# Hybrid mLSTM and S5 decoder layer: the input products of an S5 unit issued ahead of the output products of the unit before it, and the mLSTM inputs taken through DRAM

## The chip, the cores and the metric

One core of one Trainium2 chip runs the whole layer in one launch. The metric is the device time of that launch in microseconds (us). Engines are named as the profile names them: PE (TensorE, matrix products), PEld (its weight loads), DVE (VectorE), ACT (ScalarE), POOL (GpSimd), SP (SyncE, which issues the DMAs).

## The reference

A layer of a decoder with 1024 features works on 1024 prompt positions and on 32 sample positions (8 rows of 4). Cut to what the change touches, it computes:

```
a = rmsnorm(h)
x_m, z_m, o_m, i, f, x_s, z_s = split(a @ w_in)     # 512 columns each; i and f have 4
x_conv = silu(causal_conv(x_m, width 4))
q, k from x_conv; v from x_m                        # 4 heads of 128, one matrix each
hA = mlstm_chunkwise(q, k, v, i, log_sigmoid(f))    # running maximum m, matrix memory C
hA = layernorm(hA * sigmoid(o_m)); hA = (hA + skip * x_conv) * silu(z_m)
yB = Re(C . scan(lam, B . x_s)) + D * x_s           # 32 groups of 16 channels, 64 complex states
yB = gelu(yB); yB = yB * sigmoid(yB @ w_glu + b) * silu(z_s)
h  = h + concat(hA, yB) @ w_out
h  = h + sigmoid(h @ w_ple_gate) * rmsnorm(p @ w_ple)
y  = rmsnorm(h)
```

It also returns the last states of the mLSTM, of the convolution and of the S5 scan.

## The kernel before

Features stand on the partitions and positions on the free axis: 1024 + 32 = 1056 columns, cut into chunks of 256, 384 and 416. A large product is made of three f32r matmuls for each block of 128 rows (`mm3`), the weight being split into a rounded part `hi` (cast on ACT, L115) and the rest `lo` = raw - hi (L116, on the engine that `lo_engine` names). So a tile of 128 output features costs 8 x 3 matmuls for each of three chunks, 72 in all. Such tiles are called after their piece of the input projection: `ps_o`, `ps_zm`, `ps_xm`, `ps_zs`, `ps_xs`.

The program has these stages: loading and normalising the input, the `xs` tiles, the S5 stage, the transition to the mLSTM (convolution, value products), the four heads of the mLSTM, the GLU, the output projection and the gate with the final norm.

**The S5 stage** (L916 to L950). The order of PE is written by hand there (`tc.manual_schedule`); everywhere else, and on all other engines, a scheduler sets it. Eight units of four channel groups each run one after the other. `s5_in(u)` builds a table `wt` on DVE and transposes it to `WV`. `s5_out(u)` builds `cs`, multiplies it (`kp`), writes the result to DRAM (`dK`) and reads it back as the Toeplitz tile `tz`. `s5_rot(u)` makes the rotations `rtr`, `rti` on DVE. `s5_run(u)` makes the input products `vr`, `vi` (16 matmuls of 144 columns, L616), rotates and scans them on DVE (`w`, `zr`, `zi`, `v`, `xs_`), makes the output products `py` (L654 and L655) from `tz` and `xs_`, and then the GELU (`sq`, `y`) and eight DMA writes to `d_y`. Between these pieces PE takes matmuls from a filler, a generator of tiles (`o_rest`, then `zm` 0 to 3, then `xm` 0 and 1), by a count of columns: `FILL_A` after the input products, `FILL_B` after the output products, `FILL_C` at the unit's end.

In the first four units a generator for the mLSTM's gates takes a step each: `tpr` on PE, sums and running maxima on DVE, `ends` to DRAM and back as `er`, a scan `mc`, `mc` to DRAM and back as `mp`, then `M`, `nM` and `nML` on DVE, `wl` on ACT, and the transposes `tpk` and `tps` on PE. These stand at the end of unit 3 in PE's order.

**The transition and the heads.** `mtile_xm(h)` brings `xm` of head h: for h = 0 and 1 it is read back from `d_xm`, where the filler wrote it, for h = 2 and 3 it is computed on the spot. Then come the convolution (`xc`, ACT L1059 and DVE L1061), the value products `vps`, and `mlstm(h)`, which begins with `qps` (L1099) and, on POOL, with a mask added to `nmb` (L1095). `glu_w` splits the GLU's weights (`hi_g` on ACT, `lo_g` on POOL, L966). `mlstm(h)` runs over two halves, each with one `qps`, so that the fifth `qps` begins head 2. The four `zs` tiles are held back by `tc.issue_after` until the last matmul of `xm` 3; they run among the heads 1 to 3.

Of the kernel before, what the change touches and what calls it, by code (L numbers as in the profile page):

```python
# [21 lines left out]
GC = 0.044715  # L22
NEG = -1.0e30
CH = ((0, 256), (256, 384), (640, 416))
FILL_A, FILL_B, FILL_C = 16500, 3600, 4400
LOC = tuple((c, 128 * (i - b)) for i, (c, b) in enumerate(((0, 0),) * 2 + ((1, 2),) * 3 + ((2, 5),) * 4))


# [1 line left out]
def tile_hymba(ctx: ExitStack, tc: tile.TileContext, d: dict, o: list):  # L30
# [535 lines left out]
    def s5_out(u):  # L566
        gs = slice(4 * u, 4 * u + 4)
        cs = s5.tile([128, 4, 9, 16], F32, tag="cs", name="cs", bufs=2)
        table(cs, Cs, Cj, 9, gs)
        yield  # L570

        kp = pt([128, 128], "kp")
        for i in range(4):
            g = 4 * u + i
            T.matmul(kp[32 * i:32 * i + 32, :], Bs[:, g:g + 2, :].rearrange("p q c -> p (q c)"),
                     cs[:, i, 0:8, :].rearrange("p t c -> p (t c)"), start=True, stop=True)
        ks = s5.tile([128, 128], F32, tag="ks", name="ks", bufs=1)
        A.copy(ks, kp)
        V.scalar_tensor_tensor(ks[:, 0:16], dsel, Dt[:, u:u + 1], ks[:, 0:16], op0=MUL, op1=ADD)
        dma(dK[u, :, :, 128:256].rearrange("r i x -> i r x"), ks)  # L580

        tz = pxm.tile([128, 4, 128], F32, tag="xm", name="tz", bufs=2)
        k0 = dK[u, 0:1, 0:1, 16:17]
        dma(tz, bass.AP(tensor=k0.tensor, offset=k0.offset, ap=[[16, 8], [256, 64], [1, 128]]))
        yield cs, tz
# [16 lines left out]
            V.tensor_tensor(dst, dst, u3, op=op)  # L602
        return rtr, rti

    def s5_run(u, WV, cs, tz, rtr, rti):
        q0 = 2 * u
        gb = 4 * (u % 2)
        us = s5.tile([128, 4, 144], F32, tag="us", name="us", bufs=2)
        dma(us, d_us[u // 2].rearrange("s c g n -> (s c) g n")[:, gb:gb + 4])
        y2 = s5.tile([128, 4, 128], F32, tag="y2", name="y2", bufs=1)  # L610
        vr, vi = pv([128, 2, 144], "vr"), pv([128, 2, 144], "vi")
        for x, v_ in enumerate((vr, vi)):
            for q in range(2):
# [236 lines left out]


    xsm = mlc.tile([128, 4, 8, 7], F32, name="xsm")
    d_xm = dram.tile([2, 128, 1024], F32, name="d_xm")

    def xm_g(h):
        hi, lo = wtile(wcols(128 * h, 128), 8, 128, f"xm{h}")
# [10 lines left out]

    def filler():
        yield from o_rest()
        for h in range(4):  # L870
            yield from z_tile_g(512 + 128 * h, h, f"zm{h}", s5)
        for h in range(2):
            yield from xm_g(h)

    fill = filler()

# [39 lines left out]
    with tc.manual_schedule(engines={mybir.EngineType.PE}):  # L916
        gate = gates_g()
        ins = [s5_in(u) for u in range(8)]
        outs = [s5_out(u) for u in range(8)]

        prod(ins[0])
        WV = prod(ins[0])
        prod(outs[0])
        nxt = prod(outs[0])
        with tc.high_priority():
            rot = s5_rot(0)
        prod(outs[1])
        for u in range(8):
            run = s5_run(u, WV, *nxt, *rot)
            prod(run)  # L930
            if u < 7:
                nxt = prod(outs[u + 1])
                prod(ins[u + 1])
            take(FILL_A)
            prod(run)
            take(FILL_B)
            if u < 7:
                WV = prod(ins[u + 1])
                with tc.high_priority():
                    rot = s5_rot(u + 1)  # L940
            prod(run)
            if u < 6:
                prod(outs[u + 2])
            take(FILL_C)
            if u < 4:
                next(gate)
        end = s5_final()
        for n in (5000, 3000, 3000, 1 << 30):
            prod(end)
            take(n)  # L950
    lo_engine[0] = G
# [7 lines left out]
    def glu_w():  # L959
        for k in range(0, 4, 2):  # L960
# [2 lines left out]
            hi = pgw.tile([128, 2, 512], F32R, name=f"hi_g{k}")  # L963
            lo = pgw.tile([128, 2, 512], F32R, name=f"lo_g{k}")
            A.copy(hi, raw)
            G.tensor_tensor(lo, raw, hi.bitcast(F32), op=SUB)  # L966
            wg.extend((hi[:, i, :], lo[:, i, :]) for i in range(2))

    mX = {}
# [68 lines left out]
    def mtile_xm(h):  # L1038
        xm = pxm.tile([128, 1027], F32, tag="xm", name="xm", bufs=2)
        V.memset(xm[:, 0:3], 0.0)  # L1040
        if h < 2:
            dma(xm[:, 3:], d_xm[h])
        else:
            hi, lo = wtile(wcols(128 * h, 128), 8, 128, f"xm{h}")

        def evac(c, t0, n, ps):
            n8 = min(n, 1024 - t0)
            A.copy(xm[:, 3 + t0:3 + t0 + n8], ps[:, :n8])
            if c == 2:
                A.copy(xsm[:, h, :, 3:7], ps[:, 384:416].rearrange("p (b t) -> p b t", t=4))  # L1050

        V.tensor_copy(xsm[:, h, :, 0:3], scT[:, h, :].rearrange("p (b j) -> p b j", j=3))
        if h > 1:
            mtile(hi, lo, evac, "xm")
        V.tensor_copy(pcn[:, h, 0:24].rearrange("p (b j) -> p b j", j=3), xsm[:, h, :, 4:7])
        V.tensor_copy(pcn[:, h, 24:27], xm[:, 1024:1027])

# [295 lines left out]
    glu_w()  # L1353
    mlstm(0, *xmc[0])
    mlstm_first(1)
    xmc[2] = mtile_xm(2)
    sample_head(2)
    xmc[3] = mtile_xm(3)
    xm_end = last_mm[0]
    with tc.high_priority():  # L1360
        sample_head(3)
    mlstm(2, *xmc[2])
    mlstm(3, *xmc[3])
    sample_end()
# [239 lines left out]
```

## Time and profile before

| what | us |
|---|---|
| median of three runs | 690.73 (690.07 to 693.43) |
| the profiled execution | 690.1 |
| its span | 688.4 |
| PE busy | 619.6 (90% of the span) |
| DVE busy | 449.6 (65%) |
| ACT busy | 266.7 (39%) |
| POOL busy | 167.5 (24%) |

The span runs from the first to the last instruction that the profile shows; 1.7 us of the execution's own time lie around it. The busy shares are averages over stages that differ: the S5 stage runs from about 103 to 252 us, the transition to 273, the heads and the GLU to 455, the output projection and the gate to the end.

### The profile page before, as it was taken

The page shows a single profiled execution, that of the slowest core. Times are in us where ns is not written, and L with a number is a line of the kernel's source. Part 1 is how long each engine was busy: PE and PEld are TensorE (multiplying, and loading weights), DVE is VectorE, ACT ScalarE, POOL GpSimd, SP SyncE. Part 2 cuts the span into 40 slices and gives each one's busy share as a digit, 9 for nine tenths or more (in the row PEclk, how much of TensorE's full clock was granted, in tenths as well). Part 3 has the DMA queues.
Part 4 walks back from the last instruction along what each step waited for, and adds up shares of the span by engine and source line. Part 5 has one row for each costly group of instructions (what it writes and reads, how often), then busy time and mean ns, then how long its engine had stood idle before and what let it go on. Part 6 is the DMA issues. An engine that isn't in the chain of part 4 may idle for free.

```text
span 688.4 us, 11569 instructions
## 1 busy us (share of the span) xinstructions
PE 619.6 (90%) x4068; PEld 544.8 (79%) x4068; DVE 449.6 (65%) x1289; ACT 266.7 (39%) x655; POOL 167.5 (24%) x173
## 2 busy tenths in 40 slices
PE   3999997987989963899899997799999999999995
PEld 2999997976988952789798896676888876788885
DVE  4878867897899648748766688945211334556344
ACT  5653732233433243434543245345111324353232
POOL 5820200000000005434443336573110214101000
PEclk9999998998999995899999999799999999999998
DMA  8812445344444528214545257467531246313121
GB/s 278 235 46 45 116 118 130 103 121 105 74 114 118 147 52 248 62 47 131 172 142 154 78 172 221 125 199 252 188 122 62 92 167 226 119 49 122 44 80 61
DMA packets 110831, 88.43 MB, mean 128 GB/s; under 512 B 33391, under 2 KB 93443, under 8 KB 110774
## 3 DMA queue, kind: packets, MB, share of 16 engines
q1 hardware_dynamic: 110774, 87.70, 43.1%
q8 instruction: 32, 0.52, 0.3%
q14 instruction: 25, 0.20, 0.1%
HBM read 61.14 MB, written 26.54 MB: 127 GB/s over the span
## 4 chain that ended last, share of the span: by engine, by line
PE 57%; DVE 17%; DMA 14%; ACT 4%; issue 4%; SPq 2%; POOL 1%; POOLq 0%; DVEq 0%; ACTq 0%
PE po L1425 4%; PE po L1424 4%; PE po L1532 4%; PE po L1423 4%; PE po L1533 4%; PE po L1534 4%; SPq L36 2%; DVE xc L1061 2%; PE ps_o L123 2%; DMA Wraw<-in_w_out 2%; PE ps_o L125 2%; PE ps_o L124 2%; PE ps_xm L123 2%; PE ps_xm L125 2%; PE ps_xm L124 2%
## 5 line engine op out<-in xcount | busy, mean ns | idle before, releaser
L1532 PE MATMUL po<-wgh,hTh 128*128 128x512 f32 (+1 forms) x136 | 52.3, 386 | 0.3 <-ACT g_t L1535 0.3
L1534 PE MATMUL po<-wgh,hTl 128*128 128x512 f32 (+1 forms) x136 | 51.1, 380 | 0.0
L1533 PE MATMUL po<-wgl,hTh 128*128 128x512 f32 (+1 forms) x136 | 51.1, 378 | 0.0
L1426 DVE TENSOR_TENSOR xt<-xt,po 128x512 f32<-128x512 f32 x16 | 11.0, 686 | 55.7 <-PE po L1425 52.2
L123 PE MATMUL ps_o<-hi_o,aTh 128*128 128x264 f32 (+2 forms) x136 | 41.7, 307 | 0.6 <-ACT aTh L178 0.6
L124 PE MATMUL ps_o<-lo_o,aTh 128*128 128x264 f32 (+2 forms) x136 | 40.4, 298 | 1.4 <-POOL lo_o L116 1.4
L125 PE MATMUL ps_o<-hi_o,aTl 128*128 128x264 f32 (+2 forms) x136 | 40.6, 298 | 0.2 <-DVE aTl L179 0.2
L123 PE MATMUL ps_xm<-aTh,hi_xm 128*128 128x256 f32 (+2 forms) x96 | 32.4, 337 | 1.4 <-ACT hi_xm L115 1.4
L1425 PE MATMUL po<-woh,mlo 128*128 128x512 f32 x80 | 32.8, 410 | 0.0
L123 PE MATMUL ps_zm<-aTh,hi_zm 128*128 128x256 f32 (+2 forms) x96 | 32.6, 340 | 0.0
L125 PE MATMUL ps_zs<-aTh,lo_zs 128*128 128x256 f32 (+2 forms) x96 | 32.3, 337 | 0.0
L124 PE MATMUL ps_zs<-aTl,hi_zs 128*128 128x256 f32 (+2 forms) x96 | 32.3, 336 | 0.0
L123 PE MATMUL ps_xs<-aTh,hi_xs 128*128 128x256 f32 (+2 forms) x96 | 31.4, 327 | 0.9 <-ACT xs L287 0.9
L1424 PE MATMUL po<-wol,mh 128*128 128x512 f32 x80 | 32.1, 402 | 0.0
L123 PE MATMUL ps_zs<-aTh,hi_zs 128*128 128x256 f32 (+2 forms) x96 | 32.0, 333 | 0.0
L124 PE MATMUL ps_xm<-aTl,hi_xm 128*128 128x256 f32 (+2 forms) x96 | 31.9, 333 | 0.0
L1423 PE MATMUL po<-woh,mh 128*128 128x512 f32 x80 | 31.7, 397 | 0.0
L125 PE MATMUL ps_xm<-aTh,lo_xm 128*128 128x256 f32 (+2 forms) x96 | 31.7, 332 | 0.0
L124 PE MATMUL ps_xs<-aTl,hi_xs 128*128 128x256 f32 (+2 forms) x96 | 31.4, 327 | 0.0
L124 PE MATMUL ps_zm<-aTl,hi_zm 128*128 128x256 f32 (+2 forms) x96 | 31.4, 327 | 0.0
L125 PE MATMUL ps_zm<-aTh,lo_zm 128*128 128x256 f32 (+2 forms) x96 | 31.3, 326 | 0.0
L125 PE MATMUL ps_xs<-aTh,lo_xs 128*128 128x256 f32 (+2 forms) x96 | 31.2, 325 | 0.0
(594 smaller groups left out, 1970.6 us busy)
## 6 DMA issues: line engine op xcount, KB each, us to landing
xt<-in_x_prompt SPq DMA_DIRECT2D x15, 512.0 KB
Wraw<-in_w_out SPq DMA_DIRECT2D x16, 256.0 KB
Wraw<-in_w_ple_gate SPq DMA_DIRECT2D x16, 256.0 KB
d_h<-xt SPq DMA_DIRECT2D x8, 512.0 KB
h_t<-d_h SPq DMA_DIRECT2D x8, 512.0 KB
out<-g_t SPq DMA_DIRECT2D x14, 256.0 KB
mt<-d_m SPq DMA_DIRECT2D x10, 256.0 KB
d_us<-xs SPq DMA_DIRECT2D x32, 72.0 KB
```

Source lines behind the costliest of these rows:

```text
L36: nc.sync.dma_start(out, in_)
L123: T.matmul(ps, wh, xh, start=first, stop=False)
L124: T.matmul(ps, wh, xl, start=False, stop=False)
L125: last_mm[0] = T.matmul(ps, wl, xh, start=False, stop=last).ins
L1061: V.scalar_tensor_tensor(xc, xm[:, j:j + 1024], cvw[:, 4 * j + h:4 * j + h + 1], xc, op0=MUL, op1=ADD)
L1423: T.matmul(ps, mh[:, k % 4, :], hi, start=k == 4, stop=False)
L1424: T.matmul(ps, mh[:, k % 4, :], lo, start=False, stop=False)
L1425: T.matmul(ps, mlo[:, k % 4, :], hi, start=False, stop=k == 3)
L1426: V.tensor_tensor(xt[:, cs], xt[:, cs], ps, op=ADD)
L1532: T.matmul(ps[:, :b - a], hTh[i][:, k, :], hi[:, ws], start=k == 4, stop=False)
L1533: T.matmul(ps[:, :b - a], hTh[i][:, k, :], lo[:, ws], start=False, stop=False)
L1534: T.matmul(ps[:, :b - a], hTl[i][:, k, :], hi[:, ws], start=False, stop=k == 3)
```

## The change

In the S5 stage the input products of unit u+1 are put into PE's order in the middle of unit u's filler, ahead of the output products of unit u; `kp` of unit u+1 stands with them. `s5_run` gets a yield after the input products for that, and a third `us` buffer. `tz` gets a buffer of its own instead of sharing that of `xm`. All four `xm` go through `d_xm`. The filler's order is `o_rest`, `xm` 0, `xm` 1, `zm` 0 to 3, `xm` 2; `xm` 3 is computed after `mlstm_first(1)`. The three column counts change. The `zs` tiles are no longer held back. `lo_engine` stays DVE after the S5 stage, and `lo_g` moves to DVE too, so that eight `lo` of 128x1024 (`xm` 2, `xm` 3, four `zs`, two `lo_g`) leave POOL for DVE.

```diff
-FILL_A, FILL_B, FILL_C = 16500, 3600, 4400
+FILL_A, FILL_B, FILL_C = 9600, 12000, 3000
...
-        tz = pxm.tile([128, 4, 128], F32, tag="xm", name="tz", bufs=2)
+        tz = s5.tile([128, 4, 128], F32, tag="tz", name="tz", bufs=2)
...
-    def s5_run(u, WV, cs, tz, rtr, rti):
+    def s5_run(u, WV, get):
...
-        us = s5.tile([128, 4, 144], F32, tag="us", name="us", bufs=2)
+        us = s5.tile([128, 4, 144], F32, tag="us", name="us", bufs=3)
...
+        yield
+        cs, tz, rtr, rti = get()
...
-    d_xm = dram.tile([2, 128, 1024], F32, name="d_xm")
+    d_xm = dram.tile([4, 128, 1024], F32, name="d_xm")
...
         yield from o_rest()
+        for h in range(2):
+            yield from xm_g(h)
         for h in range(4):
             yield from z_tile_g(512 + 128 * h, h, f"zm{h}", s5)
-        for h in range(2):
-            yield from xm_g(h)
+        yield from xm_g(2)
...
         for u in range(8):
-            run = s5_run(u, WV, *nxt, *rot)
-            prod(run)
-            if u < 7:
-                nxt = prod(outs[u + 1])
-                prod(ins[u + 1])
-            take(FILL_A)
-            prod(run)
-            take(FILL_B)
+            prod(runs[u])
             if u < 7:
                 WV = prod(ins[u + 1])
+            take(FILL_A)
+            if u < 7:
+                start(u + 1, WV)
+                tabs = prod(outs[u + 1])
                 with tc.high_priority():
-                    rot = s5_rot(u + 1)
-            prod(run)
+                    parts[u + 1] = (*tabs, *s5_rot(u + 1))
+            if u < 6:
+                prod(ins[u + 2])
+            take(FILL_B)
+            prod(runs[u])
+            prod(runs[u])
...
-    lo_engine[0] = G
...
-            G.tensor_tensor(lo, raw, hi.bitcast(F32), op=SUB)
+            V.tensor_tensor(lo, raw, hi.bitcast(F32), op=SUB)
...
-        if h < 2:
-            dma(xm[:, 3:], d_xm[h])
-        else:
-            hi, lo = wtile(wcols(128 * h, 128), 8, 128, f"xm{h}")
+        dma(xm[:, 3:], d_xm[h])
...
+    for _ in xm_g(3):
+        pass
     xmc[2] = mtile_xm(2)
...
-    with tc.issue_after(xm_end):
-        for j in range(4):
-            zs_tile(j)
+    for j in range(4):
+        zs_tile(j)
```

Three places of the orders are shown; lines of the changed kernel lie one or two higher than those of the kernel before.

**The gates, on DVE.** `M` (with `mp`), `nM`, `nML` and `colv` are the last steps of the gates; `v`, `xs`, `rtr`, `rti`, `u` and `w` belong to an S5 unit, `sq` and `y` to a unit's GELU. Before:

```order
L601 TENSOR_TENSOR u_2689<-rBi,rAi 128x256
L782 TENSOR_SCALAR M__2013<-M__2013,mp 32x128
L553 TENSOR_TENSOR cs<-u_2233,u_2234 128x576
L663 SCALAR_TENSOR_TENSOR y_2043<-sq,py 128x256
...
L783 TENSOR_TENSOR m__2014<-M__2013,bb__2011 32x128
L785 TENSOR_SCALAR nM<-M__2013 32x128
L661 SCALAR_TENSOR_TENSOR sq<-sq,py 128x272
L551 TENSOR_TENSOR u_2359<-pdr,Bs 128x4x128
L552 TENSOR_TENSOR u_2360<-pdi,Bj 128x4x128
L790 COPY nML<-nM 32x1
```

And in the change, with SP's DMAs of the same place under it:

```order
L645 TENSOR_TENSOR xs__2329<-v_2332,v_2333 64x2x128 x2
L599 TENSOR_TENSOR rti<-rBr,rAi 128x256
L599 TENSOR_TENSOR rtr<-rBr,rAr 128x256
L646 TENSOR_TENSOR xs__2329<-v_2334,v_2335 64x2x128 x2
...
L600 TENSOR_TENSOR u_2857<-rBi,rAi 128x256
L783 TENSOR_SCALAR M__2032<-M__2032,mp 32x128
L784 TENSOR_TENSOR m__2033<-M__2032,bb__2030 32x128
L786 TENSOR_SCALAR nM<-M__2032 32x128
L791 COPY nML<-nM 32x1
```

```order
L36 DMA er_2040<-ends 4x8x2
L36 DMA d_xm<-xe 128x384
L36 DMA xm<-d_xm 128x1024
L36 DMA raw_zm_2999<-in_w_in 128x8x128
L36 DMA out<-mc 4x1
L36 DMA d_y_1067<-y_1880 16x16x32 x8
L36 DMA mp<-mc 32x1x1
```

The chain of unit 3 (`w` to `xs_`) now stands ahead of `M` on DVE: from the first `w` of unit 0 to `M` there were 119 instructions and are 154. Between `M` and `nML` eight stood and two stand. On SP `mp<-mc` used to follow `out<-mc` at once; now the eight writes of a unit's `y` are between them.

**The end of the S5 stage, on ACT.** `xe` is the evacuation of a chunk of an `xm` tile (here of `xm` 2), `xc` the first step of the convolution of heads 0 and 1, `v` the evacuation of `vps`, `ctmp` the convolution's tanh. In the change:

```order
L862 COPY xe<-ps_xm 128x384
L1059 ACTIVATE xc<-xm,hcols 128x1024
L1068 ACTIVATE csm<-xsm,hcols 128x32
L1082 COPY v_3520<-vps 128x4x128 x2
L1059 ACTIVATE xc<-xm,hcols 128x1024
L977 CAST hi_g_3728<-raw_g 128x1024
L977 CAST hi_g_3734<-raw_g 128x1024
L862 COPY xe<-ps_xm 128x384
L865 COPY xsm<-ps_xm 128x8x4
L1114 ACTIVATE nmb<-nmb,colv 128x128 x4
L1082 COPY v_3558<-vps 128x4x128 x2
L1064 ACTIVATE ctmp<-xc 128x512 x2
```

In the kernel before `xm` 2 was computed after the convolutions of heads 0 and 1; now the first `xc` follows the evacuation of the second chunk of `xm` 2 in ACT's queue.

**The third head, on PE.** `qps` and `tpxc` begin a half of a head, `ps_g` is the GLU. Before:

```order
L1149 MATMUL fps<-Cst,wk 128x129
L1099 MATMUL qps<-xc,Gm 128x512
L125 MATMUL ps_zs_5056<-aTh_105,lo_zs_5024 128x384
L1105 MATMUL tpxc<-ident,xc 128x128 x4
L123 MATMUL ps_zs_5056<-aTh_105,hi_zs_5023 128x384
L124 MATMUL ps_zs_5056<-aTl_108,hi_zs_5023 128x384
```

And in the change:

```order
L1099 MATMUL qps<-xc,Gm 128x512
L1105 MATMUL tpxc<-ident,xc 128x128 x4
L1198 MATMUL skv<-wk,sxv 96x128
L1199 MATMUL skv<-wv,sxv 96x128
L123 MATMUL ps_zs_5285<-aTh_106,hi_zs_5223 128x416
L124 MATMUL ps_zs_5285<-aTl_109,hi_zs_5223 128x416
L125 MATMUL ps_zs_5285<-aTh_106,lo_zs_5224 128x416
L123 MATMUL ps_g<-yh,hi_g_3728 128x256
```

When head 2 begins, before, more than two of the four `zs` tiles are still to come; in the change three `zs` matmuls are left, and `ps_g` stands right behind them. Further down, 25 matmuls of the output projection stand ahead of the end of the last head, where none stood.

## Rows read from the trace of the kernel before

**Rows 1.** Page, part 2: busy tenths in 40 slices of 17.2 us.

```profile
PE   3999997987989963899899997799999999999995
```

**Rows 2.** Busy time by stretch: length, PE, PEld, DVE, ACT, POOL (instructions), clock, DMA.

```profile
104.20:160.40 56.20, 49.40 (x451) 47.44 (x448) 46.44 (x118) 15.31 (x49) 0.31 (x3) 0.94 0.46 117
...
167.00:252.10 85.10, 81.57 (x589) 77.07 (x585) 71.64 (x212) 27.76 (x81) 0.31 (x3) 0.98 0.44 106
252.10:273.30 21.20, 3.78 (x17) 3.49 (x16) 13.60 (x12) 9.70 (x19) 10.00 (x4) 0.61 0.77 220
273.30:356.20 82.90, 76.47 (x522) 69.15 (x522) 59.29 (x187) 34.76 (x86) 34.74 (x29) 0.96 0.37 111
356.20:455.30 99.10, 89.81 (x646) 81.61 (x646) 78.35 (x255) 44.71 (x114) 46.84 (x47) 0.95 0.49 148
372.00:416.00 44.00, 44.00 (x319) 40.88 (x317) 31.50 (x119) 15.66 (x45) 14.41 (x15) 1.00 0.49 144
416.00:456.00 40.00, 31.48 (x234) 27.77 (x234) 33.95 (x97) 20.42 (x48) 24.56 (x24) 0.87 0.52 164
455.30:688.40 233.10, 225.14 (x1214) 176.90 (x1214) 98.55 (x178) 75.33 (x176) 41.21 (x42) 0.99 0.38 126
```

**Rows 3.** PE's waits, by what released it: us in all, times, longest.

```profile
PE vps L1081 <- DMA xm<-d_xm: 9.1, 1, 9.1
PE qps L1099 <- DVE xc L1065: 8.4, 1, 8.4
...
PE py L654 <- DMA tz<-dK: 3.9, 1, 3.9
...
PE py L655 <- DVE xs__2072 L645: 2.7, 1, 2.7
```

**Rows 4.** Timeline of the gates' last steps: start, length, what, idle before.

```profile
160.44 0.27 DVE L782 TENSOR_SCALAR M__2013<-M__2013,mp 32x128 f32<-32x128 f32 x1 [0.29 <-DMA mp<-mc]
...
164.10 3.98 SPq L36 DMA_DIRECT2D d_y<-y  x8
...
164.24 0.24 PE L797 MATMUL tpk<-ident,wl__2037 32*128 32x32 f32 x1 [2.87 <-ACT wl__2037 L792]
...
166.44 0.26 PE L806 MATMUL tps<-ident,gs 32*4 32x32 f32 x2 [1.90 <-DVE colv L798]
```

**Rows 5.** PE's timeline: first matmuls of the 256 and of the 416 chunk of `xm` 1.

```profile
235.77 0.39 PE L123 MATMUL ps_xm<-aTh,hi_xm 128*128 128x256 f32 x1
...
242.91 0.35 PE L123 MATMUL ps_xm<-aTh,hi_xm 128*128 128x416 f32 x1
```

**Rows 6.** ACT's groups from 252 to 290 us: busy us, mean ns, idle.

```profile
L1114 ACT ACTIVATE nmb<-nmb,colv 128x128 f32<-128x128 f32 x8 | 2.6, 389 | 7.0 <-POOL nmb L1095 7.0
L1059 ACT ACTIVATE xc<-xm,hcols 128x1024 f32<-128x1024 f32 x2 | 2.5, 1238 | 4.4 <-DMA xm<-d_xm 4.4
...
L1082 ACT COPY v<-vps 128x512 f32<-128x512 f32 x4 | 2.2, 562 | 0.0
...
L965 ACT CAST hi_g<-raw_g 128x1024 fp32r<-128x1024 f32 x2 | 2.0, 1038 | 0.0
```

**Rows 7.** `lo_g` on POOL, an `xc` step on DVE beside it, and one without it.

```profile
264.92 5.62 POOL L966 TENSOR_TENSOR lo_g<-raw_g,hi_g 128x1024 fp32r<-128x1024 f32 x2
...
264.94 3.40 DVE L1061 SCALAR_TENSOR_TENSOR xc<-xm,hcols,xc 128x1024 f32<-128x1024 f32 x1
...
273.81 1.27 DVE L1061 SCALAR_TENSOR_TENSOR xc<-xm,hcols,xc 128x1024 f32<-128x1024 f32 x1
```

**Rows 8.** Tile `ps_zs`: its matmuls from 355 us on, and its steps on DVE.

```profile
355.00:416.00 61.00, 35.58 (x177) 28.30 (x175) 4.61 (x9) 4.12 (x9) 1.00 0.46 136
...
L715 DVE SCALAR_TENSOR_TENSOR ztmp<-ztmp,ps_zs x12: 406/532/589, 338.5 to 407.2; 128x256 f32<-128x256 f32 x4, 128x384 f32<-128x384 f32 x4, 128x416 f32<-128x416 f32 x4
```

**Rows 9.** Tile `po` in the output projection and the gate: PE busy (matmuls).

```profile
510.00:560.00 50.00, 46.98 (x194) 35.33 (x193) 6.00 (x9) 2.05 (x8) 1.00 0.25 90
```

**Rows 10.** Busy time around the first two halves of head 0, columns as in rows 2.

```profile
261.00:289.00 28.00, 16.61 (x88) 14.12 (x89) 25.98 (x34) 11.96 (x26) 17.92 (x10) 0.65 0.59 167
```

More of the change, by code (lines that the diff above doesn't have):

```diff
@@ L919, in tile_hymba, with start @@
         outs = [s5_out(u) for u in range(8)]
+        parts = {}
+        runs = []
+        def start(u, WV):
+            runs.append(s5_run(u, WV, lambda: parts[u]))
+            prod(runs[u])
         prod(ins[0])
@@ L923, in tile_hymba @@
         prod(outs[0])
-        nxt = prod(outs[0])
+        tabs = prod(outs[0])
         with tc.high_priority():
-            rot = s5_rot(0)
+            parts[0] = (*tabs, *s5_rot(0))
+        start(0, WV)
+        prod(ins[1])
         prod(outs[1])
         for u in range(8):
-            run = s5_run(u, WV, *nxt, *rot)
-            prod(run)
-            if u < 7:
-                nxt = prod(outs[u + 1])
-                prod(ins[u + 1])
-            take(FILL_A)
-            prod(run)
-            take(FILL_B)
+            prod(runs[u])
             if u < 7:
                 WV = prod(ins[u + 1])
+            take(FILL_A)
+            if u < 7:
+                start(u + 1, WV)
+                tabs = prod(outs[u + 1])
                 with tc.high_priority():
-                    rot = s5_rot(u + 1)
-            prod(run)
+                    parts[u + 1] = (*tabs, *s5_rot(u + 1))
[3 more added lines that the diff above has]
+            prod(runs[u])
+            prod(runs[u])
             if u < 6:
@@ L1040, in mtile_xm @@
         V.memset(xm[:, 0:3], 0.0)
-        if h < 2:
-            dma(xm[:, 3:], d_xm[h])
-        else:
-            hi, lo = wtile(wcols(128 * h, 128), 8, 128, f"xm{h}")
[L1046 to L1050, printed above, removed]
+        dma(xm[:, 3:], d_xm[h])
         V.tensor_copy(xsm[:, h, :, 0:3], scT[:, h, :].rearrange("p (b j) -> p b j", j=3))
-        if h > 1:
-            mtile(hi, lo, evac, "xm")
         V.tensor_copy(pcn[:, h, 0:24].rearrange("p (b j) -> p b j", j=3), xsm[:, h, :, 4:7])
@@ L1358, in tile_hymba @@
     xmc[3] = mtile_xm(3)
-    xm_end = last_mm[0]
     with tc.high_priority():
```

## The prediction

> **What bounds the kernel now.** I read the page's busy digits first [rows 1]: PE stands at 9 in most slices, so it is the engine to keep fed, and the places with 3, 6, 7 and 8 are where time can be won. The span by stretches says how much [rows 2]: in the S5 stage after the gates (167 to 252 us) PE is busy 81.6 of 85.1 us; in the transition (252 to 273) only 3.8 of 21.2; in the first heads 76.5 of 82.9; in the last heads with the GLU (356 to 455) 89.8 of 99.1; in the output projection and the gate 225.1 of 233.1. So the transition loses 17.4 us, the last heads 9.3, and the S5 stage up to the gates' end has waits of its own. The list of PE's waits names them [rows 3]: 9.1 us for the load of `xm` from DRAM, 8.4 for the convolution on DVE, 3.9 for `tz`, 2.7 for `xs_`. The timeline adds 2.87 and 1.90 at the gates' transposes [rows 4]. The change goes for nearly all of these. The question is which wait ends last in their place. All sums are made against the profiled execution, 690.1 us, of which 1.7 lie outside its span of 688.4. It is 0.6 under the median of 690.73, and I leave that as it is. A measurement of this kernel tells about 0.5% from no change, so "same" is 687.3 to 694.2.
>
> **S5 stage up to the gates.** `tps` ends the gates at 166.44 [rows 4]. The new order takes 3.9 + 2.7 + 2.87 + 1.90 = 11.4 us of waits off PE's way there: `tz` and `xs_` have half a unit more time. The granted clock was 0.94 over 56.2 us [rows 2], about 3.4 us lost, which followed the wait for `tz`. One unit's input products more stand ahead of the gates: eight matmuls at the stretch's mean of 49.40/451 = 0.11 us, 0.9. PE alone would reach the transposes near 166.4 - 11.4 - 3.4 + 0.9 = 152.5.
>
> But the transposes need `wl`, and `wl` needs `M` on DVE, where 35 instructions more now stand ahead. DVE did 118 in 46.44 us [rows 2], 0.39 each, so the 35 cost 13.8, and a DVE that never idles comes to `M` at 104.2 + 46.4 + 13.8 = 164.4. It idled 9.8 us of the 56.2; the products it waited for come earlier now, so I keep 3: 167.4. From `M` to `tps` it took 166.44 - 160.44 = 6.0 [rows 4]; six fewer DVE instructions stand between `M` and `nML`, some 2.3 us at 0.39, and the last wait for `colv` was work of the same sort, so I take 2.9. `tps` then comes at **170.3**, 3.9 later than before: four waits become one of nearly 18 us. Bounds: 167.3 without any idle time of DVE; 179 with all 9.8 of it and 2 us for `mp`, whose DMA now stands behind eight writes of `y` on SP's queue, 3.98 us to issue [rows 4], half of which DVE's other work covers. The load of `xm` 0 that stands ahead of `mp` on SP too waits for its own write; both end before `M` is reached, so I cost it at nothing.
>
> **S5 stage after the gates.** From 166.44 to 252.1 it took 85.7. PE's idle 3.5 [rows 2] goes, since `py` no longer follows its own unit's products. Eight matmuls have moved ahead of the gates, 81.57/589 = 0.14 each, 1.1. The whole of `xm` 2 comes in. Its price: the chunks of 256 and 384 columns took 242.91 - 235.77 = 7.1 us [rows 5], 48 matmuls for 640 of 1056 columns, so the tile is 11.8, or 0.164 a matmul. 85.7 - 3.5 - 1.1 + 11.8 = 92.9, and `xm` 2 ends at 263.2.
>
> **The transition.** The first `qps` used to come at 273.3. The load of `xm` 0 and 1 is early now, so the 9.1 of [rows 3] goes. What is late next is ACT: the first `xc` stands behind the evacuation of the second chunk of `xm` 2, which PE finishes 4.7 us (the rest of 11.8 after 7.1) before its end, at 258.5. From there ACT has two `xc` of 1.24, four `v` of 0.56, two `hi_g` of 1.04 and four `nmb` of 0.39 [rows 6], 8.4, then two evacuations and a `ctmp`, for which I take the `v` row's 0.56 each, 1.7, and DVE a last step of about the same: `qps` at 258.5 + 10.6 = **269.1**. PE waits some 6 us there in place of 17.4, but it has `xm` 2 behind it. DVE's side, its `xc` steps (1.27 each undisturbed [rows 7]), fits beside that. `lo_g` on DVE costs it two more such steps, which lie beside ACT's work.
>
> The stretched rows bear on the eight `lo` that move. Beside `lo_g` on POOL (5.62 us for two) an `xc` step took 3.40 instead of 1.27 [rows 7], so DVE lost 2.1 us to a `lo` of 2.8 that itself costs about 1.3 on DVE. I book no gain, as PE bounds the stretch that follows. The Trainium skill, "SBUF — State Buffer", section "SBUF: two separate sides", says that a VectorE instruction with two SBUF inputs and a GpSimd instruction that reads SBUF lock each other out for a whole instruction. By that page DVE is freed for eight times 2.8 and pays eight times 1.3; if all of this came back to PE it could return at most the idle 6.4 us of the first heads, and the sum would be 678 instead of 685; no row shows that these 6.4 are due to it.
>
> **First heads.** From the first `qps` to the fifth it took 82.9. Of 288 `zs` matmuls 177 came after 355 [rows 8]; now all but three come before the fifth `qps`. `xm` 2, 72 matmuls, is done. So 105 matmuls more at 0.164, 17.2: 100.1, and the fifth `qps` comes at 369.2, 13 us later than before, with PE full as it was from 372 to 416 [rows 2].
>
> **Last heads and GLU.** Before, 99.1 us. PE loses 177 x 0.164 = 29.0 of its 89.8 and keeps 60.8. DVE had 78.35 and loses nine `ztmp` steps of 0.53 [rows 8], 4.8: 73.6. So DVE has more than PE here, and what is left is a chain that goes to and fro between the two. DVE's best share next to such work is 33.95 of 40.0, 0.85 (416 to 456) [rows 2]. 73.6/0.85 = **86.6**, and the stage ends at 455.8, where it ended before at 455.3: what the transition gave is spent, because the `zs` tiles, which filled PE's gaps here, have been used up. Bounds: PE's 60.8 plus the 9.3 it idled, 70.1, and DVE at the share of 372 to 416, 31.5/44 = 0.715, 102.9.
>
> **Output projection and gate.** 25 matmuls of it now stand ahead of the last head's end, in gaps of PE. One takes 46.98/194 = 0.24 [rows 9], 6.0 in all. 233.1 - 6.0 = 227.1, end at 682.9, and with 1.7 around it **684.6 us**.
>
> The other edits I cost at nothing: two more `xm` written to DRAM and read back, with the DMA engines busy less than half of the time in the stretches concerned [rows 2], and the third `us` buffer and the buffer for `tz`, which only take waits away.
>
> **The rivals.**
>
> 1. *PE stays the bound to the end.* If the heads' chains overlap with the GLU and with the output projection that now stands near, the last heads take 70.1, not 86.6: 16.5 less, **668.1**. For it: the GLU's start is no longer held by `zs`. Against: DVE's 73.6 alone exceeds it, so a part must slip behind. Chance 0.18.
> 2. *Slower: the last heads run at DVE's lower share.* Heads 2 and 3 are chains of PE, DVE and ACT steps; the fillers that hid each step's latency are gone. At 0.715 the stage takes 102.9, 16.3 more than I take: **700.9**. The point from which it decides: over 9.6 us more than forecast (684.6 to 694.2), a stage of 96.2, a share under 0.765. For it: the stretch where PE was full had just this share. Against: there PE was the bound and DVE could rest. Chance 0.13.
> 3. *The clock.* Around the first halves of head 0 PE was busy 16.6 of 28 us and the granted clock was 0.65, between the two levels of 1.2 and 2.4 GHz [rows 10]; from 416 to 456 it was 0.87 at 31.5 of 40. A PE with 60.8 us of work in 87 lies between. At 0.65 the 60.8 become 93.5, 6.9 more than the forecast's stage: **691.5**. Chance 0.12.
> 4. *The new order of the S5 stage gives nothing.* DVE keeps all its idle time and `mp` is late: `tps` at 179, 8.7 later than I take: **693.3**. PE then stands 26 us at the transposes. For it: DVE's order puts a whole unit ahead of `M`. Against: the waits for products are what kept DVE idle. Chance 0.15.
>
> **How the numbers follow.** The forecast has 0.42, of which 0.35 falls under 687.3 and 0.07 in "same". Rival 1 is all faster, 0.18. Rival 2 is slower, 0.13. Rival 3 gives 0.10 same and 0.02 slower; rival 4 gives 0.12 same and 0.03 slower. Faster 0.53, same 0.29, slower 0.18. The range has to leave out at most 0.2: from 670, which cuts about half of rival 1 (0.09), to 696, which cuts most of rival 2 (0.10). Within the forecast alone, with `tps` between 167.3 and 173 and a DVE share of 0.82 to 0.88, it is 679 to 690.
>
> **What would show it.** Right: no waits for `tz`, `xs_` or the load of `xm`; one wait of 15 to 20 us at `tpk` for `wl`, with DVE near full before it; the first `qps` near 269, released by DVE's `xc` after a full ACT; PE near 9 tenths up to about 369; then DVE at 0.85 with PE at 0.7 and a lower clock. Wrong: `tps` before 165 or after 176; PE at 9 tenths after 370 (rival 1); a stage from the fifth `qps` to the last head's end of over 96 us (rival 2).

## The result and the profile after

| | us |
|---|---|
| median of the changed kernel, four runs | 681.69 (680.70 to 683.84) |
| before, beside it, four runs | 692.08 (690.07 to 693.44) |
| ratio | 0.9856, 95% interval 0.9817 to 0.9896 |
| the profiled execution, and its span | 683.84, 682.0 |
| forecast for the profiled execution, and its span | 684.6, 682.9 |

The change makes the kernel about 1.4% faster; on another chip the same kernel gave 0.9878 (0.9854 to 0.9901; changed_again below). The execution that was profiled before is the fastest of its four and that of the change the slowest of its four, so the stages compared here show 6 of the 10 us by which the medians differ. The page of the changed kernel, its busy times and its 40 slices:

```profile
PE 619.2 (91%) x4068; PEld 543.8 (80%) x4068; DVE 439.5 (64%) x1297; ACT 267.0 (39%) x655; POOL 146.3 (21%) x165
...
PE   3999999991999994899999978779999999999995
...
PEclk9999999995999997899999989859999999999999
```

PE's work is the same (619.2 us, before 619.6), so what was won is idle time of PE. The slices that answer to [rows 1] show where: the S5 stage is filled up but for one slice (the 1 in the tenth), the transition has one slice far under 9 (the 4 in the sixteenth), and the last heads have become thinner (7, 8, 7, 7 from the 24th slice on, before 9, 7, 7, 9).

The same by stretches, columns as in [rows 2]:

```profile
104.20:169.20 65.00, 50.70 (x493) 47.41 (x493) 60.97 (x161) 20.14 (x60) 0.32 (x3) 0.90 0.49 129
169.20:263.70 94.50, 94.19 (x663) 90.15 (x663) 69.33 (x194) 35.36 (x93) 0.32 (x3) 0.98 0.38 100
263.70:272.70 9.00, 0.04 (x2) 0.02 (x1) 6.22 (x9) 3.44 (x10) 3.40 (x2) 0.61 0.86 269
272.70:368.10 95.40, 93.03 (x630) 86.97 (x631) 69.10 (x223) 41.83 (x104) 27.15 (x28) 0.96 0.46 142
368.10:454.40 86.30, 70.48 (x499) 57.96 (x497) 65.08 (x227) 39.24 (x97) 44.55 (x45) 0.90 0.55 167
454.40:682.00 227.60, 220.34 (x1186) 174.00 (x1182) 94.67 (x174) 73.03 (x171) 36.04 (x38) 0.98 0.36 121
```

After the gates PE idles 0.3 of 94.5 us. The transition is 9.0 us with PE empty. The first heads are full, the last heads idle 15.8 of 86.3. PE's longest waits, as in [rows 3]:

```profile
PE tpk L798 <- ACT wl__2056 L793: 13.7, 1, 13.7
...
PE qps L1099 <- DVE xc L1065: 9.0, 1, 9.0
PE tph L1139 <- ACT so L1173: 5.6, 2, 3.6
PE nu L1126 <- DVE Cst L1132: 3.1, 2, 2.1
```

No `tz`, no `xs_`, no load of `xm`. What the gates' last steps look like now, beside [rows 4]:

```profile
160.51 4.64 SPq L36 DMA_DIRECT2D d_y<-y  x8
165.19 0.73 SPq L36 DMA_DIRECT2D mp<-mc  x1
...
167.03 0.27 DVE L783 TENSOR_SCALAR M__2032<-M__2032,mp 32x128 f32<-32x128 f32 x1 [2.22 <-DMA mp<-mc]
...
168.42 0.31 PE L798 MATMUL tpk<-ident,wl__2056 32*128 32x32 f32 x1 [13.72 <-ACT wl__2056 L793]
...
169.18 0.26 PE L807 MATMUL tps<-ident,gs 32*4 32x32 f32 x2 [0.35 <-DVE colv L799]
```

`M` comes at 167.0, `mp` having waited on SP for eight writes of `y` (4.64 us to issue), and PE stands 13.7 us at `tpk`. DVE had been ready for `M` 2.2 us before `mp` came. Behind the wait the granted clock is 0.50 from 168.4 to 172 us and 0.74 from there to 175, which costs some 2.6 us more (an estimate from these windows: half of 3.6 and a quarter of 3.0). The first `qps` comes at 272.7, and this is what lies before it:

```profile
261.10 0.45 SPq L36 DMA_DIRECT2D nmb<-d_row  x1
...
266.11 3.00 POOL L1095 TENSOR_TENSOR nmb<-nmb,cmask 128x512 f32<-128x512 f32 x1 [48.76 <-DMA nmb<-d_row]
...
269.14 1.28 ACT L1114 ACTIVATE nmb<-nmb,colv 128x128 f32<-128x128 f32 x4 [5.28 <-POOL nmb L1095]
270.33 1.04 ACT L1082 COPY v<-vps 128x512 f32<-128x512 f32 x2
271.27 1.15 ACT L1064 ACTIVATE ctmp<-xc 128x512 f32<-128x512 f32 x2
```

ACT stands 5.28 us at the four `nmb`, whose load SP issues only at 261.10; the tanh of the convolution, which `qps` needs, is queued behind them. The load is not all of this wait: POOL's step between them took 3.00 us here, where the median of its eight is 1.30.

### The profile page after: what moved, and what is told of

It is laid out like the page before. It is cut to its first block, busy times and chain, and to the rows that moved or that the text cites. A ratio compares the mean times of both kernels' runs of the same rounds, so it can differ in the third digit from the quotient of the medians.

```text
span 682.0 us, 11600 instructions
## 1 busy us (share of the span) xinstructions
PE 619.2 (91%) x4068; PEld 543.8 (80%) x4068; DVE 439.5 (64%) x1297; ACT 267.0 (39%) x655; POOL 146.3 (21%) x165
## 4 chain that ended last, share of the span: by engine, by line
PE 62%; DVE 14%; DMA 12%; ACT 4%; issue 3%; SPq 3%; POOL 1%; POOLq 0%; ACTq 0%; DVEq 0%
PE po L1423 5%; PE po L1422 5%; PE po L1424 4%; PE po L1531 4%; PE po L1533 4%; PE po L1532 4%; SPq L36 3%; PE ps_zs L123 2%; PE ps_zs L125 2%; PE ps_zs L124 2%; PE ps_zm L123 2%; PE ps_zm L124 1%; DMA Wraw<-in_w_out 1%; PE ps_zm L125 1%; DMA raw_zm<-in_w_in 1%
## 5 line engine op out<-in xcount | busy, mean ns | idle before, releaser
L1532 PE MATMUL po<-wgl,hTh 128*128 128x512 f32 (+1 forms) x136 | 51.4, 378 | 0.0
L125 PE MATMUL ps_xm<-aTh,lo_xm 128*128 128x256 f32 (+2 forms) x96 | 33.2, 347 | 0.4 <-DVE lo_xm L116 0.4
L1422 PE MATMUL po<-woh,mh 128*128 128x512 f32 x80 | 33.2, 422 | 0.0
L1431 DVE TENSOR_TENSOR hTl<-tr,hTh 128x512 fp32r<-128x512 f32 x16 | 11.0, 690 | 30.9 <-ACT hTh L1430 30.9
```

Source lines behind the costliest of these rows:

```text
L125: last_mm[0] = T.matmul(ps, wl, xh, start=False, stop=last).ins
L1422: T.matmul(ps, mh[:, k % 4, :], hi, start=k == 4, stop=False)
L1431: V.tensor_tensor(hTl[i][:, 4 * q:4 * q + 4, :], tp, hi.bitcast(F32), op=SUB)
L1532: T.matmul(ps[:, :b - a], hTh[i][:, k, :], lo[:, ws], start=False, stop=False)
```

## The experiments

Twelve runs, each timed in five rounds against the kernel before on its chip; changed_again is the changed kernel itself. The runs stand on four chips, so runs of different chips are compared by their ratios. The first three columns are places in the profiled execution, in us; the next three are PE's gaps added up from its timeline, from 103.4 us to the first `qps`, from there to the fifth, and from there to the end.

| kernel | `tps` | first `qps` | fifth `qps` | PE idle to first `qps` | first heads | rest | span | ratio to before |
|---|---|---|---|---|---|---|---|---|
| before | 166.4 | 273.3 | 356.2 | 32.6 | 6.3 | 10.1 | 688.4 | |
| the change | 169.2 | 272.7 | 368.1 | 23.6 | 2.4 | 15.9 | 682.0 | 0.9856 |
| changed_again | 168.0 | 271.2 | 366.7 | 23.6 | 2.1 | 16.1 | 680.3 | 0.9878 (0.9854 to 0.9901) |
| s5_order_only | 169.3 | 274.4 | 357.3 | 35.1 | 5.4 | 11.6 | 690.9 | 1.0001 (0.9972 to 1.0030) |
| s5_order_early_gates | 158.8 | 266.6 | 358.3 | 27.2 | 7.3 | 13.7 | 688.4 | 0.9998 (0.9975 to 1.0022) |
| rest_only | 164.3 | 270.8 | 366.4 | 20.0 | 2.7 | 18.4 | 682.5 | 0.9926 (0.9903 to 0.9949) |
| old_order_early_gates | 161.9 | 274.6 | 370.5 | 21.9 | 3.4 | 18.5 | 683.1 | 0.9923 (0.9895 to 0.9951) |
| old_order_gates_smb_late | 161.4 | 271.4 | 357.6 | 20.5 | 2.9 | 13.6 | 675.8 | 0.9757 (0.9719 to 0.9796) |
| gates_a_unit_earlier | 155.3 | 260.7 | 355.6 | 13.8 | 1.5 | 15.1 | 667.2 | 0.9692 (0.9668 to 0.9716) |
| early_gates_and_mask | 155.8 | 257.5 | 356.4 | 10.0 | 5.1 | 16.9 | 671.7 | 0.9680 (0.9652 to 0.9708) |
| mask_after_tanh | 167.4 | 268.1 | 365.8 | 20.7 | 5.0 | 17.3 | 681.6 | 0.9866 (0.9835 to 0.9896) |
| lo_on_gpsimd | 168.5 | 270.8 | 361.6 | 22.3 | 7.2 | 15.5 | 681.3 | 0.9920 (0.9899 to 0.9941) |
| zs_2_and_3_held | 156.0 | 261.4 | 352.2 | 14.3 | 12.2 | 9.9 | 675.3 | 0.9830 (0.9797 to 0.9866) |
| more_dve_in_glu | 168.8 | 273.2 | 367.4 | 24.5 | 0.5 | 20.1 | 685.7 | 0.9933 (0.9904 to 0.9963) |

The theory (A) is that of the prediction: the new order of the S5 stage gathers PE's waits into one at the gates; the rest of the change wins in the transition; the last heads give some of it back.

**s5_order_only**: the diff of the S5 stage alone, all else as before.

> Only the S5 part of the change: input products a unit early, third us buffer, tz in its own buffer, new column counts; filler order, xm, zs and lo as before. Theory A (the early products only move PE's waits: tz, xs_, wl and colv, 11.4 us, become one wait for wl of 13 to 14 us, as in the changed kernel): tps at 168 to 171 instead of 166.4, no waits after it in the S5 stage (3.5 us), so the S5 stage ends within 2 us of 252; the transition keeps its 17 us; ratio to before 0.995 to 1.003. Rival B (the early products carry the gain): S5 stage ends 6 to 10 us earlier, ratio 0.985 to 0.991.

Measured 1.0001. PE's waits:

```profile
PE tpk L798 <- ACT wl__2056 L793: 14.4, 1, 14.4
PE vps L1093 <- DMA xm<-d_xm: 11.3, 1, 11.3
...
PE qps L1111 <- DVE xc L1077: 8.4, 1, 8.4
```

As theory A says: the one wait of 14.4 us is there, the S5 stage ends where it did, the transition keeps both its waits. The early products without the rest of the change are worth nothing.

**rest_only**: all of the change but the order of the S5 stage.

```diff
-            prod(runs[u])
+            run = s5_run(u, WV, *nxt, *rot)
+            prod(run)
...
-                start(u + 1, WV)
```

> The change without the order of the S5 stage: each unit's products in their old place with the old column counts; filler order, xm through DRAM, xm 2 in the filler, zs not held, lo on DVE as changed. Theory A: the gain is here. tps near 166 with its old four waits, xm 2 done near 264, first qps 271 to 274, end as in the changed kernel: 680 to 685 us, ratio 0.983 to 0.991. Rival B: without the early products the S5 stage takes 8 us longer than in the changed kernel: xm 2 done near 270, ratio 0.996 to 1.000.

Measured 0.9926: the larger part of the gain is here, as A has it, but not all: by the ratios 0.5 to 0.7% is missing against the changed kernel, on other chips. In the profiled executions the two are level (spans of 682.5 and 682.0), and up to the first `qps` rest_only is even 1.9 us ahead; what it lacks lies behind the fifth, where PE idles 18.4 us instead of 15.9. So the half per cent can't be put down to the S5 stage. PE's waits up to the first `qps`:

```profile
PE qps L1085 <- DVE xc L1051: 6.0, 1, 6.0
PE tpk L796 <- ACT wl__2037 L791: 4.4, 1, 4.4
PE py L653 <- DMA tz<-dK: 3.2, 1, 3.2
PE py L654 <- DVE xs__2072 L644: 1.9, 1, 1.9
```

The waits for `tz` and `xs_` are still there, one wait for `wl` of 4.4 stands for the 13.7.

**gates_a_unit_earlier**: in the changed kernel the gates' second step (`tpr` to `M`) is taken at the end of unit 0.

```diff
-            if u < 4:
+            for _ in range((2, 0, 1, 1, 0, 0, 0, 0)[u]):
                 next(gate)
```

> The changed kernel with the gates' first transposes (tpr) put at the end of unit 0 instead of unit 1; tpk and tps stay. M then stands 38 rows earlier on DVE and mp ahead of the unit's eight d_y writes. Theory A (the wait of 13.7 us at tpk is the place of M on DVE and mp on SP, and PE bounds the stage after it): the wait falls under 2 us, xm 2 ends 9 to 13 us earlier (near 252), and the end comes 7 to 12 us earlier: 670 to 675 us, ratio 0.967 to 0.976. Rival D (DVE, 60 of 63 us busy there, is the true bound and PE's wait was its slack): PE waits in py for xs_ instead, xm 2 ends 0 to 4 us earlier, ratio 0.980 to 0.986.

Measured 0.9692, a median of 669.11 us. Windows of the S5 stage, and what is left of the waits there:

```profile
103.40:155.30 51.90, 50.18 (x491) 47.03 (x489) 51.39 (x138) 19.85 (x59) 0.32 (x3) 1.00 0.48 131
155.30:251.70 96.40, 93.29 (x663) 89.61 (x663) 77.36 (x218) 35.65 (x94) 0.32 (x3) 0.98 0.45 115
```

```profile
PE tpq L844 <- ACT swl L840: 3.1, 1, 3.1
...
PE tps L807 <- DVE colv L799: 1.6, 1, 1.6
```

`tps` comes at 155.3, 13.9 us earlier than in the change, `xm` 2 is done at 251.7, 12 us earlier, and the first and fifth `qps` follow by the same 12; the span is 14.8 us shorter. So the wait was the place of `M` and `mp`, which this edit moves together, and not a lag of DVE (rival D), and PE bounds what follows. DVE is 51.4 of 51.9 us busy up to `tps`: it was just fast enough.

**old_order_early_gates**: the same edit in rest_only.

> The change without the order of the S5 stage (as in rest_only), with the gates' tpr at the end of unit 0. Theory A (the early products are worth their 8 us only where the gates don't take it back): the waits for wl and colv, 6.0 us in rest_only, go; those for tz and xs_, 7.9 us in four, and the half clock after tz stay; xm 2 is done near 259; end 676 to 680, ratio 0.978 to 0.984, 7 to 10 us above gates_a_unit_earlier. Rival E (the early gates alone carry that gain and the products' place is worth nothing): within 3 us of gates_a_unit_earlier, ratio 0.968 to 0.973.

Measured 0.9923, no gain: `tps` comes 2.4 us earlier than in rest_only, the first `qps` 3.8 later. A new wait shows, on DVE and then on PE:

```profile
182.84 0.28 DVE L1325 TENSOR_TENSOR smb<-smb,smask 32x128 f32<-32x128 f32 x1 [7.99 <-DMA smb<-d_srow]
...
184.46 1.23 PE L615 MATMUL vr<-us,WV 128*64 128x144 f32 x8 [6.43 <-ACT WV L563]
```

The earlier gates let the scheduler put a step of the sample rows, `smb`, among the units, where its DMA held DVE for 8.0 us. Neither theory had foreseen it.

**old_order_gates_smb_late**: the same with that step held on DVE.

```diff
-    V.tensor_tensor(smb, smb, smask, op=ADD)
...
+    with tc.issue_after(y_last[0]):
+        V.tensor_tensor(smb, smb, smask, op=ADD)
...
```

> As old_order_early_gates, but the two additions to smb (a mask of the sample rows) are held on DVE behind the last unit's GELU: in old_order_early_gates DVE stood 8.0 us at the first of them, for a DMA, and PE then 6.4 us for WV. Theory A: without that new wait the early gates do pay in the old order too: 6 to 8 us less than old_order_early_gates, 677 to 681 us, ratio 0.978 to 0.984. Rival H (in the old order DVE's lag takes back whatever the gates give): within 3 us of it, ratio 0.988 to 0.995.

Measured 0.9757, faster than A asked for, but not for A's reason. The first `qps` comes at 271.4, where rest_only has 270.8: in the S5 stage the gates' time went into another wait,

```profile
PE py L656 <- DVE xs__2540 L646: 5.6, 1, 5.6
PE py L655 <- DMA tz<-dK: 3.3, 1, 3.3
```

so there rival H is right: with its products in the old place a unit waits for DVE whenever PE is early. The gain lies behind, from the first `qps` on, where the scheduler made another order (571 matmuls before the fifth `qps`, in rest_only 629), with PE idle 16.5 us instead of 21.1. By the first `qps`, then, the new order is worth 271.4 - 260.7 = 10.7 us once the gates are early, with the rest of the change in place, and nothing while they are late. To the end less is left of it: the ratios, 0.9757 here and 0.9692 in gates_a_unit_earlier, lie some 4.5 us apart.

**s5_order_early_gates**: early gates in s5_order_only.

> As s5_order_only, with tpr at the end of unit 0. Theory A (the wait of 14.4 us for wl is all that hid the worth of the early products): the wait falls under 3 us, the S5 stage ends 11 to 14 us earlier, near 238, the transition keeps its 18 us, ratio 0.980 to 0.985 where it was 1.000. Rival D (the transition's loads, which stand on SP behind the writes of the last unit, or DVE, take it back): ratio 0.990 to 0.998.

Measured 0.9998. The first `qps` does come 7.8 us earlier than in s5_order_only; at the fifth 34 more matmuls are done (554 against 520, as the windows count them) but it comes 1.0 later; and the profiled end is 2.5 us earlier, the medians are level. PE idles 4 us more behind the first `qps`. Neither A nor the place that D names (the transition waits 19.6 us, and 19.7 in s5_order_only) explains the rest; that stays open. The longest new wait of PE there, 2.5 us at a `zs` tile for DVE's `ztmp`, is only a part of it.

**mask_after_tanh**: in the changed kernel the `nmb` exponentials of head 0 are held on ACT behind the convolution's tanh.

```diff
-            for c in range(4):
-                A.activation(sd[:, c, :], nmb[:, c, :], AF.Exp, ...)
+            with (tc.issue_after(ctmp_last[0]) if h == 0 else ExitStack()):
+                for c in range(4):
+                    A.activation(sd[:, c, :], nmb[:, c, :], AF.Exp, ...)
```

> The changed kernel with the exponentials of nmb of head 0 held on ACT until the convolution's tanh of head 0 is issued. Theory A (the first qps was late by 3.6 us against the forecast because ACT stood 5.3 us at these exponentials, for a load that SP issued at 261): the first qps comes at 266 to 268 instead of 272.7; then PE waits for the weights of xm 3, whose load SP issues near 271, so that the end comes only 0 to 3 us earlier. Rival F (the convolution, not the load, sets it): first qps within 1.5 us of 272.7. Rival G (PE bounds all that follows): end 4 to 6 us earlier, ratio 0.977 to 0.980.

Measured 0.9866, the same as the change. PE's waits at the place:

```profile
PE qps L1101 <- DVE xc L1067: 6.1, 1, 6.1
PE ps_xm L123 <- ACT hi_xm L115: 5.0, 1, 5.0
```

The wait before the first `qps` falls from 9.0 to 6.1 us, and the next one, for the weights of `xm` 3, grows from 2.0 to 5.0. The first `qps` lies 4.6 us earlier than in the change's profile, but 1.8 of that were there at `tps` already, so 2.8 are the edit's. A's sequence holds, F and G fall. What is left of the first wait, 6.1 us, is the convolution on DVE: the tanh is done at 264.1, but DVE's step on it starts at 267.33, behind an `xc` step, two `lo_g` (1.22 us each) and a copy (1.26). So the `lo_g` that the change gives to DVE stand in the way there.

**early_gates_and_mask** joins that edit to the early gates and takes `tpq` a unit later.

> The changed kernel with tpr at the end of unit 0, tpq a unit later (it waited 3.1 us for swl in gates_a_unit_earlier), and the exponentials of head 0 behind the tanh. Theory A: no wait over 2 us in the S5 stage, xm 2 done near 249, first qps near 253; 663 to 667 us, ratio 0.959 to 0.967. Rival: what is won up to the first qps is lost to the loads of the heads' inputs and the zs weights: 667 to 670.

Measured 0.9680 (0.9652 to 0.9708), no different from gates_a_unit_earlier: the first `qps` comes 3.2 us earlier, the fifth 0.8 later. The rival holds, and the 253 that A gave for the first `qps` was missed by 4.5.

**lo_on_gpsimd**: the `lo` behind the S5 stage back on POOL. These are seven of the eight, since that of `xm` 2 is made within the S5 stage and stays on DVE.

```diff
+    lo_engine[0] = G
     s5x.close()
...
-            V.tensor_tensor(lo, raw, hi.bitcast(F32), op=SUB)
+            G.tensor_tensor(lo, raw, hi.bitcast(F32), op=SUB)
```

> The changed kernel with the eight lo steps after the S5 stage back on GpSimd. Theory A (the move of lo is worth nothing, as booked): within 2 us of the changed kernel, ratio to before 0.983 to 0.989; PE idle in the first heads still about 2.4 us. Rival C (GpSimd's lo holds DVE up, which held PE up): xc and csm steps stretched to 2 to 3 us again, PE idle 6 to 7 us from the first to the fifth qps, 4 to 6 us slower than the changed kernel, ratio 0.991 to 0.995.

Measured 0.9920, by the ratios about 3 us behind changed_again (0.9878, another chip; the intervals just overlap); the spans of the profiled executions are level (681.3 against 682.0 and 680.3). PE idles 7.2 us in the first heads, as rival C said, in place of 2.4. But C's reason is not shown by that. No `xc` step takes more than 1.44 us in this run, and only one `csm` step is stretched to over 2; and the scheduler made another order of PE, with 550 matmuls ahead of the fifth `qps` instead of 629 and 73 `zs` matmuls behind it instead of 3. Whether the `lo` on POOL or the missing filler makes PE idle was not separated. DVE and POOL in that kernel, a `csm` step alone, and two beside a `lo`:

```profile
263.38 0.24 DVE L1071 SCALAR_TENSOR_TENSOR csm<-xsm,hcols,csm 128x32 f32<-128x32 f32 x1
...
281.58 2.35 POOL L116 TENSOR_TENSOR lo_zs<-raw_zs,hi_zs 128x1024 fp32r<-128x1024 f32 x1 [0.46 <-ACT hi_zs L115]
...
281.70 2.58 DVE L1071 SCALAR_TENSOR_TENSOR csm<-xsm,hcols,csm 128x32 f32<-128x32 f32 x2
```

The first of the two takes the length of the `lo`. The Trainium skill, "SBUF — State Buffer", section "SBUF: two separate sides", has it that a VectorE instruction with two SBUF inputs and a GpSimd instruction that reads SBUF exclude each other for the whole instruction; this row agrees.

**zs_2_and_3_held**: in gates_a_unit_earlier two of the `zs` tiles wait for head 2.

```diff
-    for j in range(4):
+    for j in range(2):
         zs_tile(j)
+    with tc.issue_after(qmm[2, 0]):
+        for j in range(2, 4):
+            zs_tile(j)
```

> gates_a_unit_earlier with zs 2 and 3 held until the first qps of head 2, so that 144 matmuls (23.6 us) go from the first heads, where PE is full, to the last heads, where it idles 13 to 15 of 80 to 85 us. Theory A (those gaps are where the change lost what it won in the transition): fifth qps 20 to 24 us earlier, last heads longer by only 13 to 18, end 4 to 8 us earlier than gates_a_unit_earlier, ratio 0.957 to 0.964. Rival I (the GLU stands behind zs on PE, and its chain with DVE then ends last): end within 3 us of it or later, ratio 0.967 to 0.975.

Measured 0.9830, 9 us slower than gates_a_unit_earlier: A is wrong here. First heads, here and there:

```profile
261.40:352.20 90.80, 78.63 (x512) 68.13 (x512) 67.44 (x225) 38.95 (x98) 29.22 (x29) 0.86 0.49 149
```

```profile
260.70:355.60 94.90, 93.36 (x630) 87.32 (x631) 70.20 (x222) 41.42 (x103) 28.05 (x28) 0.95 0.46 142
```

118 matmuls fewer made that stretch only 4.1 us shorter: PE idles 12.2 us instead of 1.5, at a granted clock of 0.86 instead of 0.95. In this order the first heads are full only because the `zs` tiles fill them. Behind the fifth `qps` it takes 11.5 us more (323.1 against 311.6), less than the 13 to 18 of A.

**more_dve_in_glu**: 16 more DVE instructions in the changed kernel's last heads, whose result nobody reads.

```diff
+                    if a == 0:
+                        extra = gl.tile([128, 256], F32, tag="extra", name="extra", bufs=1)
+                        V.scalar_tensor_tensor(extra, tg[:, a:b], 1.0, v[:, j], op0=ADD, op1=MUL)
```

> The changed kernel with one more DVE instruction of 128x256 behind each of the 16 tg steps of the GLU, which writes a tile that nobody reads: 16 of 0.54 us, 8.6 us more of DVE's work in the last heads, on no chain but DVE's own order. Theory A (DVE bounds the last heads, as the forecast's term for them has it): the end comes 6 to 9 us later than in the changed kernel, ratio to before 0.997 to 1.002. Rival J (a chain that goes to and fro between the engines bounds them, and DVE, busy 65 of 86 us there, has room): 0 to 3 us later, ratio 0.985 to 0.992.

Measured 0.9933, 3.8 us behind changed_again and 5.3 behind the first measurement of the change, between the two theories. The instruction, by its minimum, median and maximum in ns, and the last heads, as far as the first `po` behind them at 459.6:

```profile
L1024 DVE SCALAR_TENSOR_TENSOR extra<-tg,yb x16: 385/424/1343, 378.0 to 431.6; 128x256 f32<-128x256 f32 x16
```

```profile
367.40:460.00 92.60, 72.89 (x500) 60.36 (x500) 74.36 (x244) 39.15 (x97) 46.16 (x45) 0.87 0.52 156
```

The median is 424 ns and not 0.54 us, but some took over 1 us, and the sixteen together 9.5. DVE is busy 9.3 us more than the 65.1 of the change, and the stage grew by 5.9, from 86.3 to 92.2; 0.7 of that is a longer wait of PE at its end, for a load of weights (`Wraw`, 3.0 us instead of 2.3). So a good half of what DVE gets there reaches the stage's end: it is on the chain for part of the time, and not its only engine.

## Why the prediction was right, and where it was not

The forecast said 684.6 us for the profiled execution, within 679 to 690; it took 683.8. By the medians the gain is larger than forecast, 1.2 to 1.4% against 0.8%. Step by step, against the profiled execution:

- **S5 stage up to the gates**: right, in part by luck. `M` was forecast at 167.4 and came at 167.0, `tps` at 170.3 and came at 169.2. DVE's work ahead of `M` is as forecast (59.9 us against 46.4 + 13.8). But of the 3 us of idle time kept for late products less than 1 came, and 2.22 went to `mp`, which the sum had at nothing. The wait was put at nearly 18 us and is 13.7, since `tps` came 1.1 us earlier and PE arrived at 154.7 and not at 152.5: a unit has sixteen input products, and the sum took eight (1096 matmuls stand ahead of `tps`, 1080 before). That DVE's order and the place of `mp` on SP make this wait is shown by gates_a_unit_earlier, which moves both.
- **S5 stage after the gates**: right, 94.5 us against 92.9, with the idle time gone; the half clock behind the wait at `tpk`, some 2.6 us, was in no term. That the idle time goes with the products' new place is shown by pairs: from `tps` to the first `qps` it takes 103.5 us in the change and 106.5 in rest_only, and with early gates 105.3 in the new order and 110.0 in the old one.
- **The transition**: the mechanism (ACT late instead of the load of `xm`) was right, the size too small: the first `qps` at 272.7 against 269.1, a wait of 9.0 us and not of some 6. The step that failed is the sum of ACT's work, 8.4 + 1.7, which took ACT as never waiting. It waited 5.28 us for `nmb`, whose load stands on SP behind the writes of the last unit and whose step on POOL was slow. [rows 6] had the sign of it: 7.0 us that ACT idled before `nmb` for that step of POOL. mask_after_tanh takes that wait away, gets 2.8 us, and loses them to the weights of `xm` 3.
- **The eight `lo`**: I booked no gain; lo_on_gpsimd, with seven of them, is some 3 us slower by the ratios. The step in doubt is "as PE bounds the stretch that follows": with the `lo` on POOL the changed kernel idles 7.2 us in the first heads, with them on DVE 2.4. How much of that is the `lo` and how much the other order of PE stays open. The sum by the rule of the Trainium skill ("SBUF — State Buffer", section "SBUF: two separate sides"), 678, had the right sign and about double the size.
- **First heads**: forecast 100.1, measured 95.4. 105 more matmuls were forecast (177 less 72; without the three that are left it is 102) and 108 came; what failed is that the 82.9 were kept with all of their idle time. It fell from 6.3 to 2.4 us.
- **Last heads**: 86.6 forecast, 86.3 measured to the first `po` behind them, but by errors that cancel, which is luck. DVE had 65.1 us of work there and not 73.6 (28 instructions fewer than before, and not nine), and a share of 0.754 and not 0.85. Nearly all of DVE's work is done by 448.1, 80.0 us into the stage, at a share of 0.81; the 6.3 us behind that are some 40 small matmuls on PE, most of them for the sample rows, and a wait of 2.3 for the weights `Wraw`, which no term of the sum had. So DVE's pace alone was the wrong name for the bound: more_dve_in_glu shows it on the chain for a part of the time. PE had 70.5 us of work and not 60.8; 6.0 of that are the 25 matmuls of the output projection, which the sum took off the next stage and did not put on this one. The reason that I gave for the loss, that the `zs` tiles have been used up here, does not make them worth more here: held back in zs_2_and_3_held they filled 5.2 us of PE's gaps behind the fifth `qps` and opened 10.7 ahead of it.
- **Output projection and gate**: 227.6 against 227.1.

Of the rivals, PE did not stay the bound to the end (the last heads took 86.3, not 70.1), nor did they run as slow as 102.9; the clock was 0.90 there, not 0.65 (that rival's sum also divides 60.8 us by 0.65 that had been taken at 0.95). The fourth rival is half right: while the gates are late, the new order gives at most 0.7% with the rest of the change, and nothing without it. Its reason did not come: `tps` was at 169.2 and not at 179, and DVE did not keep its idle time.

So where does the gain of the change come from? Mostly from the rest (rest_only, 0.9926), where PE's idle time up to the first `qps` falls from 32.6 to 20.0 us: the wait for the load of `xm` is gone, and `xm` 2 is done ahead of it. The parts of the rest were not tried one by one, but for the `lo`. The order in the title adds half a per cent by the ratios, which the traces do not show up to the fifth `qps`, where rest_only is not behind. What pays is the gates a unit earlier in the new order: 669.1 us, 0.9692, some 13 us below the change by the ratio to changed_again, is the best version found, with early_gates_and_mask level with it. The old order with early gates comes to 0.9757, so to the end the order itself is worth 0.65% there, and not the 10.7 us of the first `qps`.

Besides the `lo`, two things stay open. Why s5_order_early_gates gives back in the heads what it wins before them; and what makes the heads of old_order_gates_smb_late shorter, where 52 `zs` matmuls are left behind the fifth `qps` and all goes faster, while 144 held on purpose made it slower. The load of `nmb` ahead of SP's last writes was not tried.

## What to carry to other kernels

When a wait is removed, price the queue of every engine between it and the next fixed point: here four waits of PE became one, because the instruction that ended it stood behind a whole unit's work on DVE and its input behind eight writes on SP, and moving its producer one unit earlier was worth more than the change. A filler is worth most where it covers latencies, so look for idle time in the stretch that it leaves before moving it to one that has gaps. And an experiment that moves one step lets a scheduler re-order the rest: read the first place at which the two traces part before believing the ratio.

## What the runs showed of the hardware

In lo_on_gpsimd a DVE step of 128x32 that takes 0.24 us alone took the 2.3 us of the `lo` that ran beside it on POOL, so in this row the loss is the length of POOL's step and not a multiple of DVE's. I had expected it from the large `xc` steps only, and these were not stretched there.
